# A decoder layer in float32: the feed-forward block with its down projection between the next block's gate and up products, and TensorE in written order

## The chip, the cores and the metric

The kernel runs on one core of a Trainium2 chip. A core has TensorE (matrix products, in the profile PE, with its weight loads PEld), VectorE (DVE), ScalarE (ACT), GpSimd (POOL) and SyncE (SP), which here only starts transfers; sixteen DMA engines move data between HBM and the on-chip memory. Products land in PSUM, eight banks of 128 x 512 float32 values. The metric is the device time of one execution in microseconds (us); less is better.

## The reference

One decoder layer on 256 tokens of width 2048. A normalised input goes through one wide projection; gated linear attention and sparse attention run on parts of it; their outputs go through an output projection and are added to the input. Then comes the feed-forward part, which is where most of the change lies (D_FF = 5632):

```python
h = x + jnp.concatenate([gla_out, nsa_out], axis=-1) @ w_out
m = rms_norm(h, ffn_norm_g)
return h + (jax.nn.silu(m @ w_gate) * (m @ w_up)) @ w_down
```

Everything is float32, and the weights are read from HBM once (210 MB are read in all).

## The kernel before

**Products in parts.** TensorE multiplies here in a reduced form of float32, so each operand is split into a high part (`hi`, a rounded copy, written by ScalarE) and a low part (`lo`, the rest, written by VectorE: `in_parts`, L598), and every product is three matmuls: high x high, high x low, low x high. The weights stream through raw buffers (`fraw`, three of 1 MB, loaded by SP) into parts buffers (`ftwo`, four, each up to 4 x 512 columns of high and of low). A parts buffer is free again when its last matmul has run.

**Blocks.** The feed-forward width is walked in eleven blocks of 512 (`fb` 0 to 10). `gate_up` (L1000) makes a block's gate and up products for all 256 tokens; it walks eight pairs of 128-row slices of the width 2048 in the order of `ORDERS`. A pair costs eight products (two slices, two token halves, gate and up), or seven where its number is in `SEVENS`: there a scheme of sums and differences, like Strassen's, saves one. The seven need three operand sums of the weights (`s1`, `s2`, L1032 to L1034, on VectorE, in `fsum` buffers, of which there are three) and four prepared forms of the tokens (`pair_forms`, made early for pairs 0, 2, 4, 5 and for 1 and 3 by `late_forms` in the first down stage). The first three products of a seven-product pair read the raw weights' parts, the other four the sums' parts. From block 2 on six pairs have seven products and two have eight. Products 1 to 7 accumulate in seven PSUM banks over all pairs, product 8 in an eighth.

**After the products.** When the last seven-product pair is through, four VectorE additions and one ScalarE copy combine four banks (L1057 to L1061); at the end of the block the remaining banks are added and the gate's silu and the product with up are made (L1070 to L1073). `turn_act` (L1079) turns the result: four transposes per half of the tokens into a bank, which `in_parts` splits; there are two halves. `down` (L1093) multiplies by `w_down`: four groups of output columns of 512, each with two token halves of twelve matmuls; the running sum `h_sb` is copied into a bank by ScalarE (L1100), accumulated on, and copied out (L1112).

**Order.** Python generators write the program: a main one (`gate_up`, `down`) yields after each product and `drive` then lets side work (`urgent`, `later`) be written, at a set pace. A planner then fixes the order on each engine: it runs the program on a model of times, and of the instructions that are ready the one written first goes first. `issue_after` (in `behind`) holds an instruction behind another on its engine. Block f's down stage comes whole, after block f+1's `gate_up`; block f's turn is side work written from the last seven-product pair of block f+1 on.

**Beginning and end.** The first projection's weight rows come in pieces from the ScalarE and SyncE queues (L176 to L183); `first_chunk` (L313) turns x by `flip` and splits the rows. The last down stage copies each finished bank out in two pieces, by ScalarE and VectorE, and stores them (L1114 to L1117).

## Time and profile before

| | |
|---|---|
| median of three runs | 1117.77 us (1116.59 to 1118.16) |
| the profiled execution: its own time | 1116.77 us |
| its span | 1115.0 us |
| TensorE busy | 1106.8 us, 99% of the span |
| VectorE busy | 935.3 us, 84% |
| ScalarE busy | 719.3 us, 65% |
| GpSimd busy | 28.8 us, 3% |
| granted TensorE clock | 1.0 of full speed throughout |
| HBM traffic | 191 GB/s over the span |

A row of the groups reads: line and engine of the instructions, operation, what is written from what, shapes, how many; behind the bar the busy time, the mean duration of one in ns, and the idle time of that engine just before them with what ended it. Durations of neighbours on one engine overlap a little, so a count times a mean is more than the busy time; for matmuls, which are pipelined, much more. The chain of waits is followed back from the last instruction: each piece is what the next one had to wait for. Tile names are the program's: `ftwo` and `fraw` as above, `f` the small buffers of the feed-forward part, `g` the larger ones.

### The profile page before, as it was taken

The numbers are of one execution on the slowest core, as the hardware profiler recorded it, in microseconds if no ns is written. First come the engines' busy times: TensorE is split into PE (matmuls) and PEld (weight loads), VectorE is DVE, ScalarE is ACT, GpSimd is POOL, SyncE is SP. The second block draws the span as 40 slices with busy tenths as digits, with TensorE's granted clock in tenths as the row PEclk, the third lists the DMA queues.
The fourth block names the chain that finished last, engine by engine and source line by source line (L and its number), as shares of the span: only waits on it lengthen the run. The fifth ranks groups of instructions, "written<-read, shape, count | busy, mean of one in ns | idle before, by whom it ended". The sixth has DMA issues, their size and how long they took to land.

```text
span 1115.0 us, 14394 instructions
## 1 busy us (share of the span) xinstructions
PE 1106.8 (99%) x5391; PEld 917.6 (82%) x5391; DVE 935.3 (84%) x1206; ACT 719.3 (65%) x957; POOL 28.8 (3%) x68
## 2 busy tenths in 40 slices
PE   9999999999999999999999999999999999999998
PEld 8888888998788887788888888888888888888886
DVE  6547679877489588999998999898999999898972
ACT  6654467544477486567676767667676767667682
POOL 3000000101000000000000000000000000000000
PEclk9999999999999999999999999999999999999999
DMA  7755543545843444575575655666474655665562
GB/s 275 235 188 189 189 152 116 171 151 165 294 171 114 145 157 165 199 244 186 188 250 166 212 195 197 205 224 212 155 260 154 235 181 191 222 226 189 182 233 76
DMA packets 110497, 213.47 MB, mean 191 GB/s; under 512 B 5157, under 2 KB 8265, under 8 KB 110426
## 3 DMA queue, kind: packets, MB, share of 16 engines
q1 hardware_dynamic: 109690, 211.18, 56.5%
q10 hardware_dynamic: 736, 1.36, 0.3%
q8 instruction: 42, 0.69, 0.2%
q14 instruction: 29, 0.24, 0.1%
HBM read 210.42 MB, written 2.10 MB: 191 GB/s over the span
## 4 chain that ended last, share of the span: by engine, by line
PE 95%; DMA 2%; ACT 1%; DVE 1%; issue 0%; ACTq 0%; DVEq 0%
PE bank L279 49%; PE bank L1013 39%; PE bank L204 2%; DMA raw<-in_w_out_dram 1%; PE bank L549 1%; PE bank L855 1%; PE bank L1086 1%; PE bank L796 1%; ACT hi L129 0%; DVE ftwo L600 0%; DVE lo L130 0%; PE bank L712 0%; DMA g<-in_attn_norm_g_dram 0%; PE bank L799 0%; PE bank L798 0%
## 5 line engine op out<-in xcount | busy, mean ns | idle before, releaser
L1013 PE MATMUL bank<-ftwo,g 128*128 128x512 f32 x1881 | 439.4, 392 | 1.0 <-DVE ftwo L600 0.8
L1013 PEld LDWEIGHTS bank<-ftwo,g 128*128 128x128 f32 x1881 | 349.3, 188 | 74.1 <-DVE ftwo L600 2.3
L279 PE MATMUL bank<-hi,g 128*128 128x512 f32 (+1 forms) x1088 | 320.2, 376 | 1.5 <-ACT hi L129 1.5
L600 DVE TENSOR_TENSOR ftwo<-fraw,ftwo 128x1536 fp32r<-128x1536 f32 (+1 forms) x130 | 263.2, 2036 | 12.7 <-ACT ftwo L599 12.0
L599 ACT ACTIVATE ftwo<-fraw 128x1536 fp32r<-128x1536 f32 (+1 forms) x130 | 221.1, 1714 | 63.5 <-PE bank L1013 28.9
L279 PE MATMUL bank<-ftwo,g 128*128 128x512 f32 x1056 | 241.6, 389 | 0.0
L279 PEld LDWEIGHTS bank<-ftwo,g 128*128 128x128 f32 x1056 | 198.1, 188 | 41.2
L279 PEld LDWEIGHTS bank<-hi,g 128*128 128x128 f32 x1088 | 190.6, 188 | 31.9 <-ACT hi L129 2.2
L130 DVE TENSOR_TENSOR lo<-raw,hi 128x1024 fp32r<-128x1024 f32 (+3 forms) x126 | 151.7, 1210 | 71.8 <-ACT hi L129 71.4
L129 ACT ACTIVATE hi<-raw 128x1024 fp32r<-128x1024 f32 (+3 forms) x126 | 131.5, 1050 | 109.4 <-PE bank L279 75.6
L279 PE MATMUL bank<-lo,g 128*128 128x512 f32 (+3 forms) x544 | 190.7, 376 | 0.3 <-DVE lo L130 0.3
L599 ACT ACTIVATE ftwo<-fsum 128x1024 fp32r<-128x1024 f32 x122 | 128.2, 1059 | 91.7 <-DVE fsum L1032 44.8
L600 DVE TENSOR_TENSOR ftwo<-fsum,ftwo 128x1024 fp32r<-128x1024 f32 x122 | 147.9, 1220 | 22.6 <-ACT ftwo L599 22.6
L279 PEld LDWEIGHTS bank<-lo,g 128*128 128x128 f32 x544 | 97.0, 189 | 15.2 <-DVE lo L130 0.8
L1032 DVE TENSOR_TENSOR fsum<-fraw 128x1024 f32<-128x1024 f32 x61 | 74.4, 1219 | 0.5 <-DMA fraw<-in_w_up_dram 0.3
L1112 ACT COPY g<-bank 128x512 f32<-128x512 f32 x80 | 45.7, 586 | 42.2 <-PE bank L279 39.9
L1100 ACT COPY bank<-g 128x512 f32<-128x512 f32 x88 | 48.3, 590 | 0.9 <-DVE g L600 0.8
L1033 DVE TENSOR_TENSOR fsum<-fsum,fraw 128x512 f32<-128x512 f32 x61 | 41.9, 687 | 0.8
L599 ACT ACTIVATE g<-bank 128x512 fp32r<-128x512 f32 x50 | 29.6, 600 | 19.2 <-PE bank L855 8.7
L1034 DVE TENSOR_TENSOR fsum<-fsum,fraw 128x512 f32<-128x512 f32 x61 | 41.8, 685 | 0.1
L204 PE MATMUL bank<-ident,g 128*128 128x128 f32 (+2 forms) x230 | 40.9, 276 | 0.1
L600 DVE TENSOR_TENSOR g<-bank,g 128x512 fp32r<-128x512 f32 x50 | 33.8, 686 | 5.5 <-ACT g L599 4.6
(206 smaller groups left out, 668.2 us busy)
## 6 DMA issues: line engine op xcount, KB each, us to landing
fraw<-in_w_down_dram SPq DMA_DIRECT2D x44, 1024.0 KB, 5.0
fraw<-in_w_gate_dram SPq DMA_DIRECT2D x86, 512.0 KB, 3.8
fraw<-in_w_up_dram SPq DMA_DIRECT2D x86, 512.0 KB, 4.7
raw<-in_w_in_dram SPq DMA_DIRECT2D x36, 1024.0 KB, 5.1
raw<-in_w_out_dram SPq DMA_DIRECT2D x16, 1024.0 KB, 5.2
raw<-in_w_in_dram SPq DMA_DIRECT2D x4, 1072.0 KB
g<-in_x_dram SPq DMA_DIRECT2D x7, 512.0 KB, 8.6
raw<-in_w_in_dram SPq DMA_DIRECT2D x2, 1056.0 KB, 9.2
```

The costliest lines, as they stand in the source:

```text
L129: act(h[:, i:i + n], r[:, k + i:k + i + n], AF.Copy)
L130: TT(o[:, i:i + n], r[:, k + i:k + i + n], f32(h[:, i:i + n]), ALU.subtract)
L204: return nc.tensor.transpose(o, i, ident[:n, :n])
L279: last["mm"] = mm(bk[t], a[:, k, t * P:(t + 1) * P], m[:, off:off + w], start=(first_ and k == 0 and i == 0), stop=(end and done), skip_gr ...
L599: act(hi, ps, AF.Copy)
L600: TT(lo, ps, f32(hi), ALU.subtract)
L1013: mm(banks[q], x, m, start=new and i == 0, stop=todo[q] == 0)
L1032: TT(s1, r[:, 1:3], r[:, 3:4].to_broadcast([P, 2, 512]), ALU.add)
L1033: TT(s2[:, 0], s1[:, 1], r[:, 1], ALU.add)
L1034: TT(s2[:, 1], s2[:, 0], r[:, 0], ALU.add)
L1100: nc.scalar.copy(banks[i][t], h_sb[2 * m + i][:, t, :])
L1112: nc.scalar.copy(h_sb[n][:, t, :], banks[i][t])
```

## The change

- From block 2 on, pairs 0 to 6 have seven products and only pair 7 eight, and the pairs are walked in their natural order. The forms for pair 6 are made late too.
- For pairs 0, 3 and 6 of these blocks `s1` no longer comes from VectorE: `added_sums` has GpSimd's queue load two weight slices into a buffer (`fadd`, two of them) and then add a third to both by an accumulating transfer; the raw load is a quarter smaller.
- Blocks 1 to 9: turn and down no longer come after the next block's `gate_up`, but between its products: the turn's first half behind product 17, its second behind product 20, and the eight halves of the down stage (one output column group, one half of the tokens, twelve matmuls, with its own bank, copy in and copy out) behind products 25, 29, 33, 37, 40, 43, 46 and 49. In block 10 only four halves are placed so, and the rest of block 9's down stage follows it.
- In these blocks every matmul and transpose is held behind the one written before it (`in_turn`), so TensorE's order is the written one.
- Buffers: four `fraw` (three), two `fsum` (three), two `fadd` (new), four `f2` (six); two of the larger buffers move to another pool.
- Beginning: the weight rows from the third on move from ScalarE's queue to SyncE's, and `first_split` puts the high part of the first row ahead of the copies of x. End: of the last output column group the first token half is finished and stored first, and the second is made in two runs of 256 columns in two banks, each stored by itself.

The diff, without the `in_turn` call in `product`, the line of `free_bank`, and the changes that only move a buffer or keep a name:

```diff
-    g4, g2, g1, small = slot(gp, "g4", 23, LINE), slot(s2p, "g2", 13), slot(s1p, "g1", 7), slot(s1p, "sm", 12)
+    g4, g2, g1, small = slot(gp, "g4", 21, LINE), slot(s2p, "g2", 13), slot(s1p, "g1", 7), slot(s1p, "sm", 12)
+    g4m = slot(s2p, "g4m", 2, LINE)
...
     first_rows(nc.sync, 1, 2)
-    first_rows(nc.scalar, 2, 3)
     first_x(nc.sync, 1)
-    first_rows(nc.scalar, 3, 4)
+    first_rows(nc.sync, 2, 3)
+    first_rows(nc.sync, 3, 4)
     x_sb.append(load_x(1))
-    first_rows(nc.scalar, 4, 6)
+    first_rows(nc.sync, 4, 6)
     first_rows(nc.sync, 6, 8)
...
-    def chunk(banks, xh, xl, ws, first_, end, parts=((0, 512),), t_first=False, onto=False, by_part=False):
-        order = [(k, i, t) for k in range(4) for t in range(NT) for i in range(3)]
+    def chunk(banks, xh, xl, ws, first_, end, parts=((0, 512),), t_first=False, onto=False, by_part=False, only=range(NT)):
+        order = [(k, i, t) for k in range(4) for t in only for i in range(3)]
         if t_first:
...
+    def first_split(turn, r, k):
+        h, o = weight("hi", 2, W0, 4), weight("lo", 2, W0, 4)
+        with behind(last.get("a")):
+            first_high = act(h[:, 0], r[:, k], AF.Copy)
+        with behind(first_high):
+            next(turn)
+        with behind(last["a"]):
+            last["a"] = act(h[:, 1], r[:, k + 1], AF.Copy)
+        with behind(last["s"]):
+            for i in range(2):
+                TT(o[:, i], r[:, k + i], f32(h[:, i]), ALU.subtract)
+        return [(h[:, i], o[:, i]) for i in range(2)]
     def first_chunk(q, res=None):
...
                 turn_rest.append((turn, r))
-                next(turn)
-                with behind(have_cols), behind(last["a"]):
-                    return split(r, 2, W0, fine=True)
+                return first_split(turn, r, 0)
             next(turn)
...
                 res = split(r, 2, W0)
+            for _ in turn:
+                pass
+            with behind(last["a"]):
+                res += split(r, 4, W0, 2)
         else:
             turn, r = turn_rest.pop()
-        for _ in turn:
-            pass
+            for _ in range(2):
+                next(turn)
+            res += first_split(turn, r, 2)
         with behind(last["a"]):
-            res += split(r, 4, W0, 2, fine=q == 0)
             squares(x_sb[q], q, ssx)
...
-    SEVENS = [(0, 2, 4), (0, 2, 4, 5)] + [(0, 1, 2, 3, 4, 5) for f in range(2, NFB)]
+    SEVENS = [(0, 2, 4), (0, 2, 4, 5)] + [(0, 1, 2, 3, 4, 5, 6)] * 9
+    ADDED = [(), ()] + [(0, 3, 6)] * 9
     EARLY = (0, 2, 4, 5)
-    LATE = {0: (1, 3)}
+    LATE = {0: (1, 3, 6)}
...
     OLD = (1, 3)
-    ORDERS = [OLD + (0, 5, 2, 4, 6, 7), (0, 1, 2, 3, 4, 6, 5, 7)] + [(0, 1, 2, 6, 3, 4, 5, 7)] * 9
+    ORDERS = [OLD + (0, 5, 2, 4, 6, 7), (0, 1, 2, 3, 4, 6, 5, 7)] + [(0, 1, 2, 3, 4, 5, 6, 7)] * 9
     forms = {}
...
         fp = ctx.enter_context(tc.tile_pool(name="fp", bufs=1, reuse_waits="tile"))
-        fw["raw"], fw["two"] = slot(fr, "fraw", 3, LINE), slot(fp, "ftwo", 4, LINE)
-        g2, small = slot(fs, "f2", 6), slot(fs, "fm", 4)
-        fw["sum"] = slot(fs, "fsum", 3, LINE)
+        fw["raw"], fw["two"] = slot(fr, "fraw", 4, LINE), slot(fp, "ftwo", 4, LINE)
+        g2, small = slot(fs, "f2", 4), slot(fs, "fm", 4)
+        fw["sum"], fw["added"] = slot(fs, "fsum", 2, LINE), slot(fs, "fadd", 2, LINE)
...
         for mat, k0, nk, c0 in parts:
-            nc.sync.dma_start(r[:, at:at + nk], mat[k0 * P:(k0 + nk) * P, c0:c0 + 512].rearrange("(k p) w -> p k w", p=P))
+            nc.sync.dma_start(r[:, at:at + nk], rows_of(mat, k0, nk, c0))
             at += nk
         return r
+    def rows_of(mat, k0, nk, c0):
+        return mat[k0 * P:(k0 + nk) * P, c0:c0 + 512].rearrange("(k p) w -> p k w", p=P)
+    def added_sums(a, c0):
+        s = fw["added"]([2, 512])
+        gb, ua, ub = (rows_of(m[0], k, 1, c0) for m, k in ((w_gate, a + 1), (w_up, a), (w_up, a + 1)))
+        nc.gpsimd.dma_start(s[:, 0:1], gb)
+        nc.gpsimd.dma_start(s[:, 1:2], ua)
+        nc.gpsimd.dma_start(s, ub.to_broadcast([P, 2, 512]), accum_op=ALU.add)
+        return s
...
-    def gate_up(fb, aTs, before):
+    def in_turn(strict, *args, **kw):
+        with behind(last.get("pe") if strict else None):
+            last["pe"] = mm(*args, **kw)
+    def gate_up(fb, aTs, before, between=None):
...
             a, b = 2 * pair, 2 * pair + 1
-            r = load4([(w_gate[0], a, 2, fb * FB), (w_up[0], a, 2, fb * FB)])
             if pair in sevens:
+                added = pair in ADDED[fb]
+                if added:
+                    s1 = added_sums(a, fb * FB)
+                r = load4([(w_gate[0], a, 2, fb * FB), (w_up[0], a, 1 if added else 2, fb * FB)])
                 w = parts_of(r[:, 0:3])
-                s1, s2 = fw["sum"]([2, 512]), fw["sum"]([2, 512])
-                TT(s1, r[:, 1:3], r[:, 3:4].to_broadcast([P, 2, 512]), ALU.add)
+                if not added:
+                    s1 = fw["sum" if ADDED[fb] else "added"]([2, 512])
+                    TT(s1, r[:, 1:3], r[:, 3:4].to_broadcast([P, 2, 512]), ALU.add)
+                s2 = fw["sum"]([2, 512])
                 TT(s2[:, 0], s1[:, 1], r[:, 1], ALU.add)
...
                 f = [tuple(forms[pair][:, i, j] for i in range(2)) for j in range(4)]
-                product(1, tokens(b, 0), w, 1)
-                yield 2
-                product(2, tokens(a, 0), w, 0)
-                yield 2
-                product(3, f[3], w, 2)
-                yield 2
-                hi_, lo_ = two_parts()
-                in_parts(hi_[:, 0:2], lo_[:, 0:2], s1)
-                in_parts(hi_[:, 2:4], lo_[:, 2:4], s2)
-                w = [(hi_[:, k], lo_[:, k]) for k in range(4)]
-                for q, x, k in ((5, f[0], 0), (7, f[2], 1), (6, f[1], 2), (4, tokens(a, 1), 3)):
+                for j, (q, x, k) in enumerate(((1, tokens(b, 0), 1), (2, tokens(a, 0), 0), (3, f[3], 2),
+                                               (5, f[0], 0), (7, f[2], 1), (6, f[1], 2), (4, tokens(a, 1), 3))):
+                    if j == 3:
+                        hi_, lo_ = two_parts()
+                        in_parts(hi_[:, 0:2], lo_[:, 0:2], s1)
+                        in_parts(hi_[:, 2:4], lo_[:, 2:4], s2)
+                        w = [(hi_[:, k], lo_[:, k]) for k in range(4)]
                     product(q, x, w, k)
                     yield 2
+                    if between is not None:
+                        yield from between.get(7 * at + j + 1, ())
             else:
-                w = parts_of(r)
+                w = parts_of(load4([(w_gate[0], a, 2, fb * FB), (w_up[0], a, 2, fb * FB)]))
                 for q, t, m in ((2, 0, 0), (3, 0, 1), (4, 1, 0), (8, 1, 1)):
...
                         yield 2
+            if between is None and before is not None and (at == 0 if free_bank else pair == last7):
+                urgent.append(before)
             if pair == last7:
...
                 TT(q57u, banks[5], q7u, ALU.subtract)
-                if before is not None:
-                    urgent.append(before)
         if fb == 0:
...
             gs.append(g)
-        turns[fb] = turn_act(gs, aTs)
+        turns[fb] = turn_act(gs, aTs, 1 if fb in WITHIN else 6 if fb else 0)
...
-    def turn_act(gs, aTs):
+    WITHIN = range(1, NFB - 1)
+    TURNS, HALVES, OVER = (17, 20), (25, 29, 33, 37, 40, 43, 46, 49), ()
+    def down_parts(f0, aTs, upto):
+        parts = {}
+        def half(n, t):
+            if t == 0:
+                parts[n] = parts_of(load4([(w_down[0], 4 * f0, 4, n * 512)]))
+            ws = parts[n]
+            ah, al = aTs[f0]
+            b = bank()
+            nc.scalar.copy(b, h_sb[n][:, t, :])
+            for k in range(4):
+                for i, (x, m) in enumerate(((ah, ws[k][0]), (ah, ws[k][1]), (al, ws[k][0]))):
+                    in_turn(True, b, x[:, k, t * P:(t + 1) * P], m, start=False, stop=(k == 3 and i == 2),
+                            skip_group_check=True)
+                yield 2
+            nc.scalar.copy(h_sb[n][:, t, :], b)
+        return [half(n, t) for n in range(upto) for t in range(NT)]
+    def turn_act(gs, aTs, gap):
         hi, lo = g4([4, S], F32R), g4([4, S], F32R)
...
             for j in range(4):
-                mm(p[:, j * P:(j + 1) * P], gs[t][:, j * P:(j + 1) * P], ident, is_transpose=True,
-                   start=(j == 0), stop=(j == 3), skip_group_check=True)
+                in_turn(gap == 1, p[:, j * P:(j + 1) * P], gs[t][:, j * P:(j + 1) * P], ident, is_transpose=True,
+                        start=(j == 0), stop=(j == 3), skip_group_check=True)
                 if j % 2:
-                    yield
+                    yield 0
             pv = p.rearrange("p (j s) -> p j s", j=4)
             in_parts(hi[:, :, ts], lo[:, :, ts], pv)
-    def down(f0, aTs, last):
+            for _ in range(gap if t == 0 else 0):
+                yield 0
+    def store(n, t, c):
+        nc.sync.dma_start(out[t * P:(t + 1) * P, n * 512 + c:n * 512 + c + 256], h_sb[n][:, t, c:c + 256])
+    def take_out(n, t, b):
+        for c in range(0, 512, 256):
+            (nc.vector.tensor_copy if c else nc.scalar.copy)(h_sb[n][:, t, c:c + 256], b[:, c:c + 256])
+            store(n, t, c)
+    def down(f0, aTs, last, ms=(0, 1)):
         todo = list(LATE.get(f0, ()))
-        for m in range(2):
+        for m in ms:
             banks = [[bank() for _ in range(NT)] for _ in range(2)]
...
                     nc.scalar.copy(banks[i][t], h_sb[2 * m + i][:, t, :])
+            if last and m == 1:
+                tail = bank()
+                nc.scalar.copy(tail[:, :256], h_sb[3][:, 1, 256:])
             for f, (ah, al) in enumerate(aTs):
...
                     ws = parts_of(load4([(w_down[0], 4 * (f0 + f), 4, n * 512)]))
+                    if last and end and n == 3:
+                        yield from chunk([banks[i]], ah, al, ws, False, end, onto=True, only=(0,))
+                        take_out(n, 0, banks[i][0])
+                        for c, b in ((0, banks[i][1]), (256, tail)):
+                            yield from chunk([{1: b[:, :256]}], ah, al, ws, False, end, ((c, 256),), onto=True, only=(1,))
+                            nc.scalar.copy(h_sb[n][:, 1, c:c + 256], b[:, :256])
+                            store(n, 1, c)
+                        continue
                     yield from chunk([banks[i]], ah, al, ws, False, end, t_first=last and end, onto=True)
...
                             continue
-                        for c in range(0, 512, 256):
-                            cs = slice(c, c + 256)
-                            (nc.vector.tensor_copy if c else nc.scalar.copy)(h_sb[n][:, t, cs], banks[i][t][:, cs])
-                            nc.sync.dma_start(out[t * P:(t + 1) * P, n * 512 + c:n * 512 + c + 256], h_sb[n][:, t, cs])
+                        take_out(n, t, banks[i][t])
...
     acts = []
+    def some(gen, n):
+        for _ in range(n):
+            yield next(gen)
+    left = []
+    def later_parts(f):
+        end = f == NFB - 2
+        turn, halves = turns[f], left + down_parts(f, acts, 2 if end else 4)
+        at = (OVER if left else ()) + HALVES
+        left[:] = halves[len(at):]
+        return {TURNS[0]: some(turn, 3), TURNS[1]: turn, **dict(zip(at, halves))}
     for f in range(NFB):
-        drive([gate_up(f, acts, turns.get(f - 1))], 2 if f == 0 else 3)
+        inner = f - 1 in WITHIN
+        drive([gate_up(f, acts, turns.get(f - 1), later_parts(f - 1) if inner else None)], 2 if f == 0 else 3)
+        drain(urgent)
         if f == NFB - 1:
             urgent.append(turns[f])
-        if f:
+            drive([down(f - 1, acts[f - 1:f], False, (1,))], 3)
+        elif f and not inner:
             drive([down(f - 1, acts[f - 1:f], False)], 3)
```

More of the change, by code (lines that the diff above doesn't have):

```diff
@@ L250, in flip @@
                     else:
-                        STT(lo[:, k, :], v, g, f32(hi[:, k, :]), ALU.mult, ALU.subtract)
+                        last["s"] = STT(lo[:, k, :], v, g, f32(hi[:, k, :]), ALU.mult, ALU.subtract)
             if q == 0:
@@ L404, in gla_gate @@
     def gla_gate(lr):
-        dec["f"], dec["r"] = g4([4, S]), g4([4, S])
+        dec["f"], dec["r"] = g4m([4, S]), g4m([4, S])
         nc.gpsimd.memset(dec["r"], 0.0)
@@ L1012, in product @@
                 todo[q] -= 1
-                mm(banks[q], x, m, start=new and i == 0, stop=todo[q] == 0)
+                in_turn(between is not None, banks[q], x, m, start=new and i == 0, stop=todo[q] == 0)
         def tokens(k, t):
@@ L1020, in gate_up @@
         last7 = max(sevens, key=order.index)
+        free_bank = all(pair in sevens for pair in order[:order.index(last7)])
         todo = dict.fromkeys((1, 5, 6, 7), 3 * len(sevens))
```

## The prediction, before the result was known

> **What bounds the kernel now.** I read the page first, then busy time by stretches, then the chain of waits, then the groups of one block. The page gives the span against which everything below is summed:
>
> ```profile
> span 1115.0 us, 14394 instructions
> ```
>
> The busy time of each engine over three stretches (microseconds, then the number of instructions; the last columns are granted clock, DMA share, GB/s):
>
> ```profile
> core 0: us, PE busy (x) PEld busy (x) DVE busy (x) ACT busy (x) POOL busy (x), PEclk, DMA share, GB/s
> 506.58:528.34 21.76, 21.76 (x97) 18.02 (x97) 21.69 (x29) 15.08 (x21) 0.00 (x0) 1.00 0.46 156
> 528.34:568.79 40.45, 40.45 (x183) 33.29 (x183) 39.87 (x39) 28.43 (x28) 0.00 (x0) 1.00 0.62 208
> 568.79:631.01 62.22, 62.22 (x280) 51.37 (x279) 58.85 (x55) 43.45 (x46) 0.00 (x0) 1.00 0.60 203
> ```
>
> The third row is one whole feed-forward block: TensorE is busy for all of it, VectorE for 58.85 of 62.22 us (94.6%), ScalarE for 70%. TensorE is the bound and VectorE is close behind. The chain of waits through that block is TensorE alone:
>
> ```profile
> 568.79 21.76 PE bank L279 x96
> 590.55 34.71 PE bank L1013 x153
> 625.26 0.22 PE bank L1086 x2
> ```
>
> A 512-wide matmul therefore costs 21.76 / 96 = 0.2267 us (34.71 / 153 says the same), one product of three matmuls 0.680, a transpose 0.11, and the eight transposes of a block 0.88. A block has 174 gate/up matmuls, 96 down matmuls and 8 transposes: 270 x 0.2267 + 0.88 = 62.09 of the 62.22. Nothing is left to gain by waiting less; only fewer matmuls can help, and only while VectorE and ScalarE keep pace. Their groups in this block:
>
> ```profile
> L600 DVE TENSOR_TENSOR ftwo<-fsum,ftwo 128x1024 fp32r<-128x1024 f32 x12 | 14.6, 1220 | 2.9 <-ACT ftwo L599 2.9
> L600 DVE TENSOR_TENSOR ftwo<-fraw,ftwo 128x2048 fp32r<-128x2048 f32 x6 | 13.6, 2287 | 0.3 <-ACT ftwo L599 0.2
> L599 ACT ACTIVATE ftwo<-fsum 128x1024 fp32r<-128x1024 f32 x12 | 12.6, 1060 | 7.7 <-DVE fsum L1032 3.0 <-DVE fsum L1034 3.0 <-PE bank L1013 1.2
> L599 ACT ACTIVATE ftwo<-fraw 128x2048 fp32r<-128x2048 f32 x6 | 11.4, 1914 | 2.7 <-DMA fraw<-in_w_down_dram 1.8 <-PE bank L1013 0.9
> L600 DVE TENSOR_TENSOR ftwo<-fraw,ftwo 128x1536 fp32r<-128x1536 f32 x6 | 10.5, 1752 | 0.0
> L599 ACT ACTIVATE ftwo<-fraw 128x1536 fp32r<-128x1536 f32 x6 | 8.9, 1486 | 3.4 <-PE bank L1013 1.9 <-DMA fraw<-in_w_up_dram 1.5
> L1032 DVE TENSOR_TENSOR fsum<-fraw 128x1024 f32<-128x1024 f32 x6 | 7.3, 1219 | 0.0
> L1112 ACT COPY g<-bank 128x512 f32<-128x512 f32 x8 | 4.6, 586 | 4.7 <-PE bank L279 4.3
> L1100 ACT COPY bank<-g 128x512 f32<-128x512 f32 x8 | 4.4, 588 | 0.0
> L1033 DVE TENSOR_TENSOR fsum<-fsum,fraw 128x512 f32<-128x512 f32 x6 | 4.1, 686 | 0.1
> L1034 DVE TENSOR_TENSOR fsum<-fsum,fraw 128x512 f32<-128x512 f32 x6 | 4.1, 685 | 0.0
> ...
> L600 DVE TENSOR_TENSOR g<-bank,g 128x512 fp32r<-128x512 f32 x3 | 2.1, 689 | 0.1
> L1073 DVE SCALAR_TENSOR_TENSOR f<-f,rf,f 128x512 f32<-128x512 f32 x2 | 1.5, 746 | 0.0
> L1072 DVE TENSOR_TENSOR f<-bank,f 128x512 f32<-128x512 f32 x2 | 1.4, 683 | 0.0
> ```
>
> The means overlap a little: with twelve small instructions of about 0.70 a block's means add to 62.8 against 58.85 busy, so each of the 55 counts about 0.07 less than its mean.
>
> **The removed product.** In blocks 2 to 10 a seventh pair goes from eight products to seven: 9 x 3 x 0.2267 = **-6.1 us**. A block that never waits then takes 62.20 - 0.68 = 61.5 us. This is the only large gain.
>
> **What VectorE pays for it.** A seven-product pair costs means of 1.752 + 1.219 + 0.686 + 0.685 + 2 x 1.220 = 6.78, an eight-product pair 2.287. The change adds one of the first, takes one of the second, and moves three of the 1.219 sums to GpSimd's transfers: +6.78 - 2.29 - 3.66 = +0.83, with two instructions more (-0.14): 59.55 of 61.5 us, 97%. The second stretch above ran at 39.87 of 40.45 without a wait, so 97% is possible in itself; what matters is when it falls due. ScalarE gains 1.49 + 2 x 1.06 - 1.91 = 1.7 us, still 73%.
>
> **The order within a block.** Before, each down stage let VectorE work ahead: 4 parts of 2.29 in 21.76 us. Now the first 25 products come without any down work between them: 25 x 0.68 + 0.88 = 17.9 us to the first half. From the end of the block before's last seven-product product, 8.2 us earlier (the last half 2.72, eight products 5.44), VectorE owes by then the evacuation and gate arithmetic and the turn (twelve at about 0.70: 8.4), four pairs (2 x 6.78 + 2 x 5.56 = 24.7) and the first down part (2.29): 35.4 in 35 instructions, 32.9 us after the overlap, in 26.1 us. So 6.8 must have been done earlier. There are four parts buffers, and for the earlier summed pairs only two sum buffers. I find room ahead for one raw part, a pair's second sum and another's first: 1.68 + 1.23 + 1.15 = 4.1. The lower end of the wait is 0 (the planner finds other work to bring forward), the upper end 6.8 - 4.1 = **2.7 us a block**.
>
> **The turn with one bank.** Seven banks are held by products, so the turn has the eighth alone: its second half, behind product 20, waits until ScalarE and VectorE have emptied the first, behind product 17. The rows of the turn before, and one of ScalarE riding on a release:
>
> ```profile
> 612.40 1.49 ACT L599 ACTIVATE ftwo<-fraw 128x1536 fp32r<-128x1536 f32 x1 [0.26 <-PE bank L1013]
> ...
> 626.72 0.38 PE L1086 MATMUL bank<-ident,f 128*128 128x128 f32 x2
> ...
> 627.14 0.60 ACT L599 ACTIVATE g<-bank 128x512 fp32r<-128x512 f32 x1 [0.38 <-PE bank L1086]
> ...
> 627.86 0.68 DVE L600 TENSOR_TENSOR g<-bank,g 128x512 fp32r<-128x512 f32 x1
> ```
>
> The second transpose starts at about 626.83 and the bank is free at 628.54: 1.7 us with both engines at hand. The three products between give 2.04 + 0.11 = 2.15, a slack of 0.4. Written order means that everything on TensorE stands behind a late transpose. The transpose's copies wait for whatever ScalarE and VectorE have begun: half of the sum of squared durations over 62.2 us gives a mean wait of about 0.4 on ScalarE and 0.64 on VectorE. 1.04 - 0.4 = 0.65 late. Worse, product 17 is the last reader of its pair's raw part, and the 612.40 row shows ScalarE starting the next part at once on such a release; a down part (1.91) would then hold ScalarE some 1.4 instead of 0.4, and the turn is 1.65 late. Ends 0 and 1.65; nearest is the average case, and I take 0.8.
>
> **The halves.** Each of the eight uses that same bank: copy out 0.59, copy in 0.59, about 0.3 of signalling, 1.5 in all, against 2.72 (four products) or 2.04 (three). The slack of 0.5 at the four close positions is passed when ScalarE is inside a 1.49 or 1.91 pass: I take 0.3 a block, ends 0 and 1.2. The copies are otherwise the same 16. Strict order by itself adds no instruction. All three causes draw on the same lateness, so they are not added at their upper ends: **1.1 us a block, 9.9 us for nine**, ends 0 and 2.7.
>
> The Trainium skill ("Perfetto Trace Analysis", Matmuls) says that independent matmul groups should rotate through different PSUM banks so that one's evacuation overlaps the next's matmuls. The change gives turn and halves one bank; by that rule the sum lies at the waiting end, which is also where these rows put it. The same page (Optimization Strategy) says that regimes with different most-contended engines may gain from interleaving; by that rule alone the sum is the first rival's below.
>
> **The sums by transfer.** No accumulating transfer stands in the trace. There are two buffers for three such pairs a block, so each can be asked for some 20 us ahead; it costs nothing unless three transfers take longer. The other end is a wait of a few microseconds a block, within the 2.7.
>
> **Beginning, end, block 1.** The first part of the first weight row goes ahead of the x copies on ScalarE:
>
> ```profile
> 6.47 0.54 ACT hi L129
> 7.01 0.04 issue
> 7.05 2.27 PE bank L279 x16
> ```
>
> At best the 0.54 and the DMA issues ahead of it leave this chain (-1.0), at worst ScalarE stands for the row and the copies are late by as much (+0.5): **-0.4**. At the end the last bank is emptied in two pieces one behind the other:
>
> ```profile
> 1111.11 0.37 ACT L1116 COPY g<-bank 128x256 f32<-128x256 f32 x1 [2.40 <-PE bank L279]
> 1111.51 0.81 SPq L1117 DMA_DIRECT2D out_dram<-g  x2
> 1111.51 0.42 DVE L1116 COPY g<-bank 128x256 f32<-128x256 f32 x1 [2.35 <-ACT g L1116]
> ```
>
> The second (0.44) goes; 24 matmuls of 256 columns in place of 12 of 512 cost 0 (half price) to 0.68 (at 2.27 / 16 each): **-0.1**, ends -0.44 and +0.24. A third late form in the down stage after block 1 (groups of that stage):
>
> ```profile
> L961 DVE TENSOR_TENSOR f<-g,g 128x512 f32<-128x512 f32 x2 | 1.4, 686 | 0.0
> ...
> L921 DVE TENSOR_TENSOR f<-f,f 128x128 f32<-128x128 f32 x2 | 0.6, 290 | 0.0
> ```
>
> 0.69 + 4 x 0.29 + 0.69 = 2.5 less overlap, 2.1 us, in the first stretch above, where VectorE already fills 21.69 of 21.76. It is covered if two pairs are ready ahead (0), else 2.1: **+0.9**.
>
> **Sum.** 1115.0 - 6.1 + 9.9 - 0.4 - 0.1 + 0.9 = 1119.2. The profiled execution took 1116.77, 1.8 more than its span: 1121.0; the median of the runs, 1117.77, lies 1.0 above that execution: **1122**. With s for the wait in a block the time is 1112.1 + 9s.
>
> **Rivals.** (1) *No wait.* The planner places the turn's copies and parts so that TensorE never stands: s = 0, 1112. For it: the second stretch ran with VectorE at 98.6% and TensorE full. Against: the slack of 0.4 at the turn. It stays faster up to s = 0.38. (2) *Break-even.* s near 0.6, the average turn alone: 1117.5; within 0.2% from 0.38 to 0.87. (3) *VectorE falls behind by the ledger*, s = 2.7: 1136. For it: the 6.8 us that have to be ahead; against: parts are also due a little after the product begins. (4) *The accumulated sums arrive late*, so the change does not relieve VectorE: some 2 us a block, 1130; against it the 20 us ahead.
>
> **Chances.** Forecast (s from 0.87 to 2) 0.34, rival 3 0.12, rival 4 0.04; break-even 0.17; no wait 0.33. A measurement of this kernel can tell about 0.2% (2.2 us) from no change: faster 0.33, same 0.17, slower 0.50. The range holds both signs, 1110.5 to 1135; the forecast's own is 1119.5 to 1130.
>
> **What would show it.** Right: blocks of 62 to 63.5 us with one TensorE gap between the products behind 17 and the transposes behind 20, ended by the turn's VectorE part; VectorE at 95% or over. Wrong: blocks of 61.5 with TensorE full (rival 1); gaps before products of pairs 2 and 3, ended by sums or parts (3); waits on GpSimd's transfers (4). 27 matmuls of 0.2267 must be gone in any case.

## The result and the profile after

The changed kernel takes 1132.18 us (median; 1131.41 to 1133.97), the one before 1117.87 us beside it (1116.59 to 1118.16). The ratio is 1.0136, 95% interval 1.0124 to 1.0149: 14.3 us **slower**. The forecast was 1122 us, slower, in a range of 1110.5 to 1135. The direction was right; the loss is more than three times the one forecast (4.2 us), and above the forecast's own 1119.5 to 1130.

The execution that was profiled took 1133.97 us, the longest of its kernel; its page gives the span, and then busy time, share and instructions of each engine:

```profile
span 1132.3 us, 14624 instructions
...
PE 1111.5 (98%) x5376; PEld 912.3 (81%) x5376; DVE 949.6 (84%) x1229; ACT 733.6 (65%) x978; POOL 93.1 (8%) x149
```

TensorE runs 5376 matmuls and transposes. Before it was 5391; 27 less for the removed products and 12 more for the two runs of 256 columns at the end give exactly that, so the work did go. Yet TensorE's busy time is 4.7 us longer than the 1106.8 before. One feed-forward block in busy time by stretches, columns as in the prediction:

```profile
core 0: us, PE busy (x) PEld busy (x) DVE busy (x) ACT busy (x) POOL busy (x), PEclk, DMA share, GB/s
613.16:677.27 64.11, 62.65 (x276) 50.51 (x276) 60.22 (x57) 44.87 (x47) 7.11 (x9) 1.00 0.75 234
```

A block takes 64.11 us where it took 62.22. From the first of the nine turns of these blocks to the last, by the starts of their first transposes, it is 512.7 us (541.23 to 1053.90) where it was 497.7: 15.0 us of the span's 17.3. Without a wait it would be 267 x 0.2267 + 0.88 = 61.41 us: **2.70 us a block are lost**. Where, is read from the timeline of TensorE over the same stretch (start, us, then the run of like matmuls and the idle time before it):

```profile
613.16 21.35 PE L1032 MATMUL bank<-ftwo,g 128*128 128x512 f32 x92 [0.80 <-DVE ftwo L617]
635.08 34.30 PE L1032 MATMUL bank<-ftwo,g 128*128 128x512 f32 x150 [0.56 <-ACT bank L1130]
669.22 0.60 PE L1032 MATMUL bank<-ident,f 128*128 128x128 f32 x4
669.57 2.69 PE L1032 MATMUL bank<-ftwo,g 128*128 128x512 f32 x9
672.13 0.66 PE L1032 MATMUL bank<-ident,f 128*128 128x128 f32 x4
672.54 3.92 PE L1032 MATMUL bank<-ftwo,g 128*128 128x512 f32 x16
677.27 0.96 PE L1032 MATMUL bank<-ftwo,g 128*128 128x512 f32 x3 [0.80 <-DVE ftwo L617]
```

Each run should last its count times 0.2267, and the next start when it ends. 613.16 + 92 x 0.2267 = 634.02, but the next starts at 635.08: 1.06 lost in and after it. In the same way 150 matmuls lose 0.13, the nine between the transposes 0.52 (671.61 against 672.13), the sixteen behind them 1.10 (676.17 against 677.27); the transposes come out 0.12 quicker than 0.11 each. The sum is 2.69. So there are **three places in the block**, and the seven blocks behind the first of the nine have all three:

- 1.10 inside the first half of the down stage, behind its first matmul (16 matmuls are five products and that one): the second needs the low part, which VectorE writes.
- 0.52 at the turn. By the starts of the single matmuls, 0.36 of it stand inside product 20, the last before the transposes: its second matmul, too, waits for a low part. The transposes themselves wait for the turn's copy for 0.1.
- 1.06 before 635.08, most of it (0.73) ahead of the fifth half (behind product 40, the first of the close positions), which waits for its bank's copy-in. The third half waits for its own, 0.16 with what follows.

Behind each stop the next spacing of two matmuls is 0.11 wider as well. Counted to the causes, this gives **1.4 us a block for VectorE's parts** (0.36 and 1.07), **1.0 for the halves' bank and 0.1 for the turn's copy**; the rest is scatter. The waits of TensorE by line and cause (total us, times, longest) name the first place and the last; eight of the nine in each row are these:

```profile
PE bank L1032 <- DVE ftwo L617: 7.1, 9, 0.8
PE bank L1032 <- ACT bank L1130: 4.7, 9, 0.6
```

VectorE around the turn, from its timeline:

```profile
670.26 1.22 DVE L617 TENSOR_TENSOR ftwo<-fsum,ftwo 128x1024 fp32r<-128x1024 f32 x1
671.39 0.69 DVE L617 TENSOR_TENSOR g<-bank,g 128x512 fp32r<-128x512 f32 x1
671.99 0.68 DVE L1073 TENSOR_TENSOR fsum<-fadd,fraw 128x512 f32<-128x512 f32 x1
672.59 1.22 DVE L617 TENSOR_TENSOR ftwo<-fadd,ftwo 128x1024 fp32r<-128x1024 f32 x1
673.73 0.69 DVE L617 TENSOR_TENSOR g<-bank,g 128x512 fp32r<-128x512 f32 x1
674.33 0.68 DVE L1074 TENSOR_TENSOR fsum<-fsum,fraw 128x512 f32<-128x512 f32 x1
674.93 2.29 DVE L617 TENSOR_TENSOR ftwo<-fraw,ftwo 128x2048 fp32r<-128x2048 f32 x1
```

It has no idle time in these rows. The turn's copy (`g<-bank,g`, 671.39) stands behind a part of the pair's own products, and the transposes start when it ends, at 672.13. But that part (670.26) ends at 671.48, product 20 waits for it and goes on at 671.53 with two more matmuls, so the transposes could not have started before 672.09. The low part of the first down weights (674.93) starts late behind five other instructions and ends at 677.22, when TensorE goes on. ScalarE at the third place:

```profile
632.57 0.59 ACT L1136 COPY g<-bank 128x512 f32<-128x512 f32 x1 [1.27 <-PE bank L1032]
633.05 1.49 ACT L616 ACTIVATE ftwo<-fraw 128x1536 fp32r<-128x1536 f32 x1
634.44 0.59 ACT L1130 COPY bank<-g 128x512 f32<-128x512 f32 x1
```

Between the copy-out of the fourth half and the copy-in of the fifth it makes a raw part of 1.49 us, and the half starts when the copy-in has ended. The chain of waits through this block is no longer TensorE alone (of its smaller pieces some are left out):

```profile
613.16 19.32 PE bank L1032 x83
...
635.08 7.79 PE bank L1032 x33
...
647.54 1.75 DVE ftwo L617
...
667.36 3.66 DVE ftwo L617 x3
671.39 0.69 DVE g L617
...
675.01 2.21 DVE ftwo L617
677.27 19.30 PE bank L1032 x83
```

Up to 642.87 it is TensorE's, but for the gap ahead of the half; from 647.54 to 677.27, almost half of the block, it runs through VectorE. The page gives the shares of the chain in the whole execution, where TensorE had 95% before:

```profile
PE 69%; DVE 20%; issue 6%; ACT 3%; DMA 1%; ACTq 0%; SPq 0%; DVEq 0%
```

### The profile page after: what moved, and what is told of

It reads as the page before. It is cut to its first block, busy times and chain, and to the rows that moved or that the text cites. A ratio compares the mean times of both kernels' runs of the same rounds, so it can differ in the third digit from the quotient of the medians.

```text
span 1132.3 us, 14624 instructions
## 1 busy us (share of the span) xinstructions
PE 1111.5 (98%) x5376; PEld 912.3 (81%) x5376; DVE 949.6 (84%) x1229; ACT 733.6 (65%) x978; POOL 93.1 (8%) x149
## 3 DMA queue, kind: packets, MB, share of 16 engines
q0 software_dynamic: 11664, 28.32, 10.9%
## 4 chain that ended last, share of the span: by engine, by line
PE 69%; DVE 20%; issue 6%; ACT 3%; DMA 1%; ACTq 0%; SPq 0%; DVEq 0%
PE bank L281 34%; PE bank L1032 28%; DVE ftwo L617 12%; PE bank L206 2%; ACT ftwo L616 2%; DVE fsum L1073 1%; DVE fsum L1074 1%; DVE g L617 1%; PE bank L566 1%; PE bank L872 1%; DVE f L1110 1%; DVE fsum L1071 1%; PE bank L813 1%; DVE f L1111 1%; DVE f L1099 0%
## 5 line engine op out<-in xcount | busy, mean ns | idle before, releaser
L1032 PE MATMUL bank<-ftwo,g 128*128 128x512 f32 x2670 | 622.0, 392 | 13.0 <-DVE ftwo L617 7.1
L132 DVE TENSOR_TENSOR lo<-raw,hi 128x1024 fp32r<-128x1024 f32 (+2 forms) x122 | 148.8, 1225 | 69.8 <-ACT hi L131 69.1
L131 ACT ACTIVATE hi<-raw 128x1024 fp32r<-128x1024 f32 (+2 forms) x122 | 129.0, 1064 | 107.1 <-PE bank L281 76.5
L617 DVE TENSOR_TENSOR ftwo<-fsum,ftwo 128x1024 fp32r<-128x1024 f32 x106 | 129.0, 1218 | 0.8 <-ACT ftwo L616 0.8
L616 ACT ACTIVATE ftwo<-fadd 128x1024 fp32r<-128x1024 f32 x34 | 35.9, 1055 | 34.5 <-DVE fadd L1071 19.6
L281 PE MATMUL bank<-ftwo,g 128*128 128x512 f32 (+1 forms) x252 | 55.5, 380 | 0.0
L1074 DVE TENSOR_TENSOR fsum<-fsum,fraw 128x512 f32<-128x512 f32 x70 | 48.1, 688 | 1.2
L1071 DVE TENSOR_TENSOR fsum<-fraw 128x1024 f32<-128x1024 f32 x36 | 43.9, 1219 | 0.3
L1014 POOL DMA_DIRECT2D fadd<-in_w_up_dram x27 | 33.2, 1231 | 129.6 <-DMA fadd<-in_w_up_dram 100.2
L617 DVE TENSOR_TENSOR ftwo<-fadd,ftwo 128x1024 fp32r<-128x1024 f32 x34 | 41.4, 1217 | 1.3 <-ACT ftwo L616 1.3
```

The source lines that it names most:

```text
L131: act(h[:, i:i + n], r[:, k + i:k + i + n], AF.Copy)
L132: TT(o[:, i:i + n], r[:, k + i:k + i + n], f32(h[:, i:i + n]), ALU.subtract)
L281: last["mm"] = mm(bk[t], a[:, k, t * P:(t + 1) * P], m[:, off:off + w], start=(first_ and k == 0 and i == 0), stop=(end and done), skip_gr ...
L616: act(hi, ps, AF.Copy)
L617: TT(lo, ps, f32(hi), ALU.subtract)
L1014: nc.gpsimd.dma_start(s, ub.to_broadcast([P, 2, 512]), accum_op=ALU.add)
```

## The experiments

All edits are made to the changed kernel, if nothing else is said. The theory: in an order that TensorE may not leave, three lates (VectorE's parts, the turn's one bank, the halves' one bank) each stop it. The rivals: the seventh pair's work on VectorE alone costs it; the bank alone; the place of the turn; the written order itself; the beginning.

**Without interleaving.** Turn and down stage go back to their old place, in the planner's order. By this edit block 9's down stage makes only its second half of the columns: 48 matmuls are left out, 48 x 0.2267 = 10.9 us.

```diff
-    WITHIN = range(1, NFB - 1)
+    WITHIN = range(0)
```

> The changed kernel with the interleaving alone undone: turn and down come whole after the next block's products again, as side work and in the planner's order; seven seven-product pairs, sums by transfer, buffers, beginning and end stay. The changed kernel takes 1132.2 us, and its block 64.1, of which 2.6 us are gaps on TensorE. If the interleaving and its one bank make the gaps, the block falls towards 61.5 and the time to 1110 to 1115. If the seventh pair's work on VectorE is too much wherever the down stage stands, gaps stay and the time is 1122 or more.

Measured: 1128.26 us, ratio 1.0086 (1.0065 to 1.0107); with the missing matmuls about 1139. One block by stretches, and TensorE's largest wait:

```profile
702.00:766.60 64.60, 63.05 (x275) 50.34 (x275) 59.98 (x57) 44.63 (x48) 7.14 (x9) 1.00 0.76 231
```

```profile
PE bank L1032 <- ACT ftwo L616: 12.1, 28, 0.6
```

The block is a little longer than the changed kernel's though nothing is interleaved and nothing ordered; many small waits, the largest sum of them for ScalarE's parts, take the place of three. So the interleaving is not what makes the seventh pair dear: with its buffers and transfers it costs more than it saves (64.60 against 62.22) without it too.

**Two banks for turn and halves.** Product 6 is accumulated in product 5's bank, so that a bank is free (the sums of these two products are mixed by that).

```diff
+            if q == 6 and between is not None:
+                banks[6] = banks[5]
```

> The changed kernel, but in blocks 2 to 10 product 6 accumulates in the bank of product 5 (so these sums are mixed and the block's result is another); every instruction stays, and turn and halves have two banks in place of one. One-bank theory: the gaps at the turn (0.55 us a block in the trace) and ahead of a half (0.84) go, together some 1.4 a block: 1132 - 9 x 1.4 = about 1120; if the bank is the cause of all, 1110. VectorE theory: the 1.07 us gap inside the first half stays or takes up what the others give back: 1128 to 1132.

Measured: 1122.98 us, 1.0048 (1.0033 to 1.0063). The gaps ahead of the halves are gone, the block takes 63.1 us, and this wait stays:

```profile
PE bank L1032 <- DVE ftwo L617: 8.4, 10, 0.9
```

So does the loss at the turn:

```profile
665.55 2.75 PE L1032 MATMUL bank<-ftwo,g 128*128 128x512 f32 x9
668.13 0.60 PE L1032 MATMUL bank<-ident,f 128*128 128x128 f32 x4
```

665.55 + 9 x 0.2267 = 667.59, so 0.54 are lost where it was 0.52. Most of it (0.43) is again product 20, which goes on at 667.56, behind a low part that ends at 667.51; the transposes wait for nothing now. So the bank is worth 9 us, 1.0 a block, and this stood ahead of the halves, not at the turn. The other two places are VectorE's, and they have grown a little, from 1.4 to 1.6 us a block.

**Less for VectorE.** Pairs 0 to 3 of blocks 2 to 10 do without their last weight sum and its parts (their seventh product takes the sum before it).

```diff
-                TT(s2[:, 1], s2[:, 0], r[:, 0], ALU.add)
+                if n2 == 2:
+                    TT(s2[:, 1], s2[:, 0], r[:, 0], ALU.add)
```

> The changed kernel, but in blocks 2 to 10 pairs 0 to 3 leave out the last weight sum and its parts (product 4 reads the parts of the sum before, so the result is another): 4 x 1.2 = 4.8 us less for VectorE and 4 x 0.5 less for ScalarE ahead of the first half; all matmuls stay. VectorE theory: the gap inside the first half (1.07 us a block) goes, and with it part of the turn's: block 62.2 to 63.0, 1115 to 1122. One-bank theory: only the VectorE gap moves to the next use of the bank: block 63.5 to 64, 1127 to 1132.

Measured: 1148.81 us, 1.0279 (1.0264 to 1.0295): **slower** by 16.6 with less work, which neither side expected. TensorE's largest wait, and the timeline of all engines at the turn of one block:

```profile
PE bank L1032 <- DVE g L617: 22.8, 9, 2.8
```

```profile
740.98 1.92 ACT L616 ACTIVATE ftwo<-fraw 128x2048 fp32r<-128x2048 f32 x1 [0.42 <-ACT ftwo L616]
...
742.81 0.57 ACT L616 ACTIVATE g<-bank 128x512 fp32r<-128x512 f32 x1
742.99 2.28 DVE L617 TENSOR_TENSOR ftwo<-fraw,ftwo 128x2048 fp32r<-128x2048 f32 x1
745.19 0.68 DVE L617 TENSOR_TENSOR g<-bank,g 128x512 fp32r<-128x512 f32 x1
...
745.92 0.66 PE L1032 MATMUL bank<-ident,f 128*128 128x128 f32 x4 [2.50 <-DVE g L617]
```

VectorE is no longer late, so the down stage's first part is started on ScalarE (740.98) and on VectorE (742.99) ahead of the turn's copies, which have just become due. The bank is empty at 745.87, and the second transposes start 2.5 us late. The gap inside the first half is gone, the one ahead of the fifth half has stayed. This is what the prediction called the worse case of the turn, on both engines.

**Both.** The two edits together.

> Both of the edits before: two banks for turn and halves, and 4.8 us less for VectorE ahead of the first half. If these two account for the gaps, TensorE does not stand in the blocks: 61.5 a block, 1132 - 9 x 2.6 = 1109. If written order itself costs (a lateness elsewhere that stops all of TensorE), the block stays at 62 or more: 1114 and over.

Measured: 1110.73 us, 0.9939 (0.9924 to 0.9954). One block:

```profile
660.00:721.47 61.47, 61.47 (x277) 50.89 (x276) 55.42 (x53) 42.99 (x48) 7.15 (x9) 1.00 0.79 243
```

TensorE has no gap; 61.47 is the 61.41 without a wait. So the −6.1 us of the removed products is real, and bank and VectorE between them hold the whole loss. Less work on VectorE helps where the bank is not single (63.1 to 61.47) and harms where it is (64.1 to 65.3 and more).

**The old beginning.** Rows from ScalarE's queue, no `first_split`; the rest is the changed kernel.

```diff
-    first_rows(nc.sync, 2, 3)
+    first_rows(nc.scalar, 2, 3)
...
-                return first_split(turn, r, 0)
+                next(turn)
+                with behind(have_cols), behind(last["a"]):
+                    return split(r, 2, W0, fine=True)
```

> The changed kernel with the beginning of before (weight rows on ScalarE's queue, copies of x ahead of the first row). In the changed kernel the first matmul of a weight starts at 8.34 us (7.05 before), and the first down stage ends 1.5 us later than before. If the new beginning costs what the trace shows, 1132.2 - 1.5 = 1130.7; if the lateness is made up by the transfers that follow, 1132; the prediction had the new beginning 0.4 cheaper: 1132.6.

Measured: 1132.1 us, 1.0132 (1.0116 to 1.0147), against 1.0136: no difference that can be seen. The beginning has no part in the loss, as far as these runs can tell.

**The turn earlier**, behind products 14 and 18 (one more product between its halves).

```diff
-    TURNS, HALVES, OVER = (17, 20), (25, 29, 33, 37, 40, 43, 46, 49), ()
+    TURNS, HALVES, OVER = (14, 18), (25, 29, 33, 37, 40, 43, 46, 49), ()
```

> The changed kernel with the turn behind products 14 and 18 in place of 17 and 20: four products between its halves (2.72 us against the 1.7 the bank needs), and product 14 releases a sums' part, not a raw part. If the turn costs only its own gap, 0.55 us a block go: 1127. If the turn's place sets what VectorE does ahead of the first half, the gap inside that half moves too: 1116 to 1124. If VectorE is behind wherever the turn stands, 1130 to 1132.

Measured: 1131.75 us, 1.0132 (1.0111 to 1.0153). The block still takes 64.1, with waits in the same places:

```profile
PE bank L1032 <- DVE ftwo L617: 5.6, 9, 0.7
PE bank L1032 <- ACT bank L1130: 4.5, 8, 0.6
PE bank L1032 <- DVE g L617: 3.6, 8, 0.4
```

What the first place loses less, the turn loses more, and now it is the transposes that wait for the turn's copy. The 0.68 us more slack did not help: the turn's place is not the cause.

**More even halves**, turn behind 14 and 18, and a fourth sum by transfer in a block (pairs 0, 2, 4, 6 for 0, 3, 6).

```diff
-    TURNS, HALVES, OVER = (17, 20), (25, 29, 33, 37, 40, 43, 46, 49), ()
+    TURNS, HALVES, OVER = (14, 18), (21, 25, 29, 33, 37, 41, 45, 49), ()
```

> The changed kernel with four products between all its halves (behind 21, 25, 29, 33, 37, 41, 45, 49), the turn behind 14 and 18, and the sums of pairs 0, 2, 4 and 6 by transfer (one pair more, 1.15 us of VectorE): the same result. One-bank theory: the slack of the bank is 1.0 us or more everywhere, so its gaps (0.55 + 0.84) go: at most 1120. VectorE theory: the first half comes four products earlier, so VectorE is 2.7 us more behind less 1.15: the gap inside the first half grows to some 2.6, and the time stays at 1130 to 1136. Both together with the other's gap gone would be 1112, below the kernel before.

Measured: 1133.76 us, 1.0148 (1.0131 to 1.0165).

```profile
PE bank L1032 <- ACT bank L1130: 10.4, 9, 1.3
PE bank L1032 <- DVE g L617: 4.7, 9, 0.7
```

The wait for VectorE's parts shrinks (1.4 us in all, three times, in the list; 0.45 a block by the starts of the single matmuls), and the bank's waits grow by as much. A better spacing alone does not pay; the run changes three things at once, so which of them moved the waits stays open.

**The planner's order on TensorE.** The interleaving stays, the holding of each matmul behind the one written before it goes.

```diff
-        with behind(last.get("pe") if strict else None):
+        with behind(None):
```

> The changed kernel without the written order on TensorE: the planner may put other ready matmuls first; nothing else changes. If written order makes TensorE stand where other work was ready, the block falls by up to the 2.6 us of gaps: 1110 to 1125. If the next matmuls would wait for the same VectorE and the same bank anyway, 1129 to 1135.

Measured: 1119.05 us, 1.0014 (1.0004 to 1.0023). One block by stretches, and TensorE's timeline at its turn:

```profile
676.94:739.38 62.44, 62.44 (x277) 50.44 (x276) 60.33 (x57) 44.27 (x48) 7.15 (x9) 1.00 0.76 240
```

```profile
727.00 0.60 PE L1032 MATMUL bank<-ident,f 128*128 128x128 f32 x4
727.35 2.93 PE L1032 MATMUL bank<-ftwo,g 128*128 128x512 f32 x11
730.12 0.60 PE L1032 MATMUL bank<-ident,f 128*128 128x128 f32 x4
```

VectorE, ScalarE and GpSimd do the same work (60.33 against 60.22 us on VectorE), but TensorE makes 11 matmuls between the transposes in place of 9, and in the trace some later products stand ahead of the first half. This takes back 13 of the 14.3 us. What is left is 1.0 us a block (62.44 against 61.41), 0.7 of it in ten wide spacings, five of them 0.335 to 0.384 for 0.2267 us. They are four short stops, which the list of waits does not hold: two matmuls start 0.05 us behind the end of a low part of VectorE's (at 729.25 and 755.38 in the block from 727.00 on), two as closely behind the copy into the bank of a half (at 739.32 and 761.90). So the same two causes are left, each much smaller, and their 1.0 us is somewhat more than the 0.68 that the removed products save: the change gains nothing.

**Free order with less for VectorE**, the edits of the third experiment and of the last.

> Free order on TensorE, and pairs 0 to 3 of blocks 2 to 10 without the last weight sum and its parts (another result; 4.8 us less for VectorE a block). With free order alone the block was 62.4 us where its matmuls and transposes need 61.5, VectorE 60.3 busy. If VectorE is what still binds, the 0.9 go: 1119.1 - 9 x 0.9 = 1111, as with two banks and written order. If the single bank binds, it stays near 1119.

Measured: 1122.03 us, 1.0035 (1.0021 to 1.005), a block of 62.65.

```profile
667.49 5.06 PE L1032 MATMUL bank<-ftwo,g 128*128 128x512 f32 x21
672.39 0.60 PE L1032 MATMUL bank<-ident,f 128*128 128x128 f32 x4
```

Again not faster. There are 21 matmuls now between the transposes: where the ordered form with this edit stood for 2.5 us, the free order puts other products. 1.2 us a block are left (62.65 against 61.41), and no longer for VectorE: of the six short stops in the block from 667.14 on, five (at 681.32, 686.53, 690.90, 696.53 and 702.58) come 0.05 us behind the copy into the bank of a half. VectorE's amount of work is not what binds here; for the most part (0.9 of the 1.2) the one bank is.

**Free order with two banks.**

> Free order on TensorE, and product 6 in the bank of product 5 (another result), so that turn and halves have two banks. If the one bank still costs in free order, 1111 to 1115; if VectorE binds and the bank is hidden by the products that the planner puts ahead, 1117 to 1120.

Measured: 1112.94 us, 0.9969 (0.996 to 0.9979), a block of 61.8. The bank is worth 0.0045 of the time, some 5 us, in the free order too, and with it the time falls below the kernel before; but two products share their sums in it.

**More sums by transfer in free order.** Four (pairs 0, 2, 4, 6), and five (0, 1, 3, 4, 6, with three buffers for them and three raw buffers):

```diff
-    ADDED = [(), ()] + [(0, 3, 6)] * 9
+    ADDED = [(), ()] + [(0, 2, 4, 6)] * 9
```

> Free order on TensorE, and the sums of pairs 0, 2, 4 and 6 by transfer in place of 0, 3 and 6: the same result, 1.15 us less for VectorE a block. If VectorE binds, most of the 0.9 us a block go: 1111 to 1115, below the kernel before. If the additional transfers (some 5% more traffic) or their landing bind, 1117 to 1122.

> Free order on TensorE, sums of pairs 0, 1, 3, 4 and 6 by transfer, three buffers for them and three raw buffers in place of four: the same result, 2.3 us less for VectorE a block. If VectorE binds and the transfers keep up, 1110 to 1113. GpSimd's queue needs about 7 us for a pair and 13 us from asking to landing, and two of these pairs follow each other twice: if the sums arrive late, 1120 to 1140.

Measured: 1124.59 us, 1.0073 (1.0061 to 1.0085), and 1138.43 us, 1.0195 (1.0168 to 1.0222), against 1.0014 with three. Five, with a raw buffer less, are irregular, with blocks of 62.5 to 68.5 us and waits of up to 4.4 us for copies into a bank that three do not have. Less for VectorE is once more not faster. With four, the block is 63.15 us, in small spacings that the list of waits does not hold. By the starts of the single matmuls, five of the seven short stops in one block come 0.05 us behind the copy into the bank of a half, and two behind a part of ScalarE's. ScalarE there:

```profile
747.62 0.59 ACT L1136 COPY g<-bank 128x512 f32<-128x512 f32 x1 [0.38 <-PE bank L1032]
748.10 1.49 ACT L616 ACTIVATE ftwo<-fraw 128x1536 fp32r<-128x1536 f32 x1
749.49 0.59 ACT L1130 COPY bank<-g 128x512 f32<-128x512 f32 x1
```

It is the third place of the changed kernel again: a part between copy-out and copy-in. TensorE goes on at 750.13, when the copy-in has ended. No version that computes the whole layer was faster than the kernel before; of those run, the free order comes nearest.

## Why the prediction was right and where it was wrong

**The bound.** Right: only fewer matmuls help, "and only while VectorE and ScalarE keep pace". They do not: the chain has moved to VectorE for half of each block.

**The removed product, −6.1.** Right, shown twice: by the count of 5376, and by the 61.47 us of a block without waits (61.5 was forecast).

**VectorE's bill.** 59.55 us a block was forecast, 60.22 measured, in the 57 instructions that the working gives (55 + 2); the overlap of neighbours was put a little too high. Its share is 60.22 / 64.11 = 94%, just under the 95% named, because the block became longer.

**The size of the waits: the step that failed.** The prediction named all three, the turn (0.8), the halves (0.3) and the parts that VectorE owes ahead of the first half (0 to 2.7), and then put: "All three causes draw on the same lateness, so they are not added at their upper ends: 1.1 us a block". 1.1 is the turn and the halves alone; the ledger of 6.8 owed against 4.1 of room got nothing. The block shows 1.4 for VectorE's parts (forecast 0), 1.0 for the halves' bank (0.3) and 0.1 for the turn (0.8). The two large ones are paid in places of the block one behind the other, so **they add**; what TensorE loses at one hardly made the next one free (with the bank's 1.0 gone, VectorE's grew by 0.2). That each has its own cause is shown by the runs: a second bank takes the gaps ahead of the halves and leaves those of VectorE's parts, less work on VectorE takes away the latter and leaves the former, and the two edits together take all. By the prediction's own formula 1112.1 + 9s the measured time is s = 2.23 over all terms, above the forecast's own case (0.87 to 2) and short of rival 3 (2.7). The sign given for rival 3 is there, though: product 20 is of pair 2, the first half stands in pair 3, and both gaps end with a part. So the sign of the change came out right with the largest term left out and another at an eighth of its forecast, and the range, which held both signs, says little for the working.

**"Strict order by itself adds no instruction."** True, and misleading: it was weighed as no cost, yet without it the same work on the same engines is 13 us quicker. What was missing is that an order that TensorE may change hides a late copy behind other products, 11 or 21 matmuls for 9, and a fixed one turns each into idle time. The prediction said that everything stands behind a late transpose, but priced only the transpose.

**The turn.** In the changed kernel it costs 0.1 of the 0.8: the sign that was given, one gap ahead of the second transposes ended by the turn's part, is hardly there, and the 0.52 that stand near are mostly product 20's own wait. The worse case was seen rightly, a part begun on a release ahead of the turn's copies. Freed of some work, VectorE and ScalarE take it, at 2.5 us where 1.65 was the upper end, as a part stands in the way on VectorE too (2.28) and not on ScalarE alone.

**The halves.** "The slack of 0.5 at the four close positions is passed when ScalarE is inside a 1.49 or 1.91 pass": the rows at 633.05 and 635.08 are this, at the first close position of eight of the nine blocks. An average was taken for what comes back in the same place each time.

**The sums by transfer.** Right: TensorE waits for none. The transfers' issues (KB each, median us to landing):

```profile
fadd<-in_w_up_dram POOLq DMA_DIRECT2D x27, 512.0 KB, 7.3
fadd<-in_w_gate_dram POOLq DMA_DIRECT2D x27, 256.0 KB, 4.4
```

A plain load and the accumulating one are about 12 us in a row, within the 20 us ahead. Rival 4 falls for three sums.

**Beginning, end and late form, +0.4 in all.** Too small to be told: the old beginning gives the same time. The first down stage ends at 529.66 us here and at 528.18 before, and between 527.68 and 531.70 in the other kernels with the same beginning and the same buffers, so 1 us either way cannot be told. With both edits, where TensorE does not stand in the blocks, the time is 1110.73; the formula gives 1112.1 at s = 0, so these terms cannot be far out together.

**Rotating banks, and interleaving.** The Trainium skill ("Perfetto Trace Analysis", Matmuls) has independent groups rotate through different banks; the runs agree, with 9.2 us in the written order (1132.18 to 1122.98) and some 5 in the free one, though a second bank gained nothing at the turn. The gain that the same page of the Trainium skill (Optimization Strategy) sees in interleaving is there as well: 62.44 us a block against 64.60 for the whole down stage in one piece, both in free order and with the seventh pair; in the written order little of it is left (64.11).

**Open.** With four sums by transfer and with less work on VectorE, TensorE in free order stops behind five copies into the halves' bank in a block where it stopped behind two; why the order falls so was not followed further. No run takes the seventh pair back and leaves the rest, so what it costs without its buffers and transfers is not known. A second bank without mixing two products was not tried, since all eight are in use.

## What to carry to other kernels

Before an order is fixed by hand on the engine that binds, list what each of its instructions waits for and add the lates that stand in different places: they need not share one price, and here a free order hid 13 of the 14 us. A single buffer that busy engines empty and fill can be late in the same place in every turn of the loop, by a long instruction that is let in between (here 1.49 us between copy-out and copy-in). When TensorE stands near such a place, look at the single matmuls before putting it down to the buffer: at the turn it was the product ahead of it that waited. Taking work off the engine behind may move another instruction ahead of the urgent one; in the written order it paid once the second bank was there, and not before.

## What the runs showed that was not expected

Less work on VectorE made the kernel slower in three pairs of runs, though in the second by so little that the intervals touch: 1132.18 to 1148.81 us in the written order; in the free order, from 1119.05 to 1122.03 without four weight sums, and to 1124.59 with one more by transfer.

A wait of TensorE has a small tail: in the starts of the single matmuls, the second spacing behind each gap is 0.335 us and not 0.227, another 0.11 us for each stop. Four of the ten wide spacings of a block in the free order are of this size.

The first 16 matmuls of a weight take quite different times in profiles of the same beginning. In the changed kernel:

```profile
7.44 3.78 PE L281 MATMUL bank<-hi,g 128*128 128x256 f32 x16 [1.67 <-ACT g L251]
```

The granted clock there, from 7.05 to 12.00 us, is 0.66. But in the twelve runs of the experiments it is 1.00, and six of these, with the same beginning, show 3.62 to 3.91 us all the same; five show 2.63 to 2.65. With the old beginning, in the kernel before and in the run that brings it back, it is 2.27. So the granted clock does not explain the difference, and what does, no run shows.
